# Two-layer hybrid decoder trunk: the first layer's x in buffers of its own, loaded by ScalarE's and GpSimd's queues

## The chip, the core and the metric

The kernel runs on one core of one Trainium2 chip. The metric is the device time of one execution in microseconds (us). Before the change three runs gave 2683.25 us as their median (2682.66 to 2684.56).

The core's engines are TensorE (PE; its weight loads are shown as PEld), VectorE (DVE), ScalarE (ACT), GpSimd (POOL) and SyncE (SP). Each executes its own instructions in the order that the program fixed, and they wait for each other by semaphores. A transfer (DMA) is issued by an engine's queue and moved by 16 DMA engines that all queues share.

## What is computed

Two decoder layers on a residual stream x of 256 tokens by 2048 features, float32:

```
for l in range(DEPTH):
    mix = hybrid_mixer(x, ...)                      # w_in projections: u, q, k, v, two gates
    x = layer_norm(DEEPNORM_ALPHA * x + mix, ...)   #   branch A: differential attention, 8 heads, causal
    h = square(relu(x @ w_mlp_up[l])) @ w_mlp_down[l]   # branch B: diagonal complex SSM, then GLU
    x = layer_norm(DEEPNORM_ALPHA * x + h, ...)     #   merged = gate_a * (attn @ w_attn_up) + gate_s * (ssm @ w_ssm_up)
```

Products are made in a split form. Each float32 operand becomes a high part, rounded to the matmul's type, and a low part, the remainder; a product is the sum of high x high, high x low and low x high.

## The kernel before

**Weights.** A weight chunk is 256 rows by 512 columns (512 KB). `load` (L331) takes a raw buffer from a ring of 4 (`RAW_BUFS`), issues the transfer on SyncE's queue (L337), and lets `split` (L141) make two tiles of it: `whi` on ScalarE (L142) and `wlo`, which needs `whi`, on VectorE (L144). `whi` and `wlo` come from rings of 3 (`HL_BUFS`), so the split of chunk n waits until TensorE has finished chunk n-3. `load_next` does this for the next chunk of a fixed plan.

**The first x.** The transposed x arrives as four pieces `c` of 512 features (512 KB each); piece 0 is cut into three transfers. Before the change, each piece took a buffer of the same ring of 4 raw buffers and the transfers stood on SyncE's queue, alternating with the first weight chunks (L422 to L431). `split` turns a piece into a tile `xT`, high on ScalarE, low on VectorE. The first projection (`gemm_feat`, L533, matmuls in L544 to L546) works through 8 weight chunks; chunks 2c and 2c+1 need piece c. A chunk is 24 matmuls.

**Background work.** Generators (`bg`) are pumped between chunks: tables for rotary embedding and SSM parameters (`rope_gen`, `ssm_param_gen`), the SSM scan (`ssm_gen`) and attention (`attn_gen`, L772). Small inputs are loaded by a list `drip` (L436), one transfer on GpSimd's queue for each finished chunk (L459).

**Attention's end.** `attn_gen` works on four pairs of heads. For each pair TensorE transposes the probabilities (L811), ScalarE copies them (`wT`, L812), TensorE multiplies with v (L817 to L819), ScalarE squares and sums (L823), VectorE makes an inverse root in some ten small operations (L825 and `rsqrt`, L319 to L327), ScalarE scales (L830), TensorE transposes back (L835), and the result is split into `ahl`: high on ScalarE (L838), low on VectorE (L839). Two pairs share an `ahl` tile. Behind the gates' projection, `w_attn_up` (`gemm_tok`, matmuls in L469, L470, L473) reads `ahl`: of the 4 chunks of each 512 output columns, the last needs the fourth pair. A chunk is 12 matmuls here.

**What sets the order.** The code above emits instructions; the order of each engine's list is then fixed by a list scheduler in the build, which works with its own model of the engines and can put an instruction ahead of ones that were emitted earlier. What is emitted early in the program can so move what stands much later.

Of the kernel before, what the change touches and what calls it, by code (L numbers as in the profile page):

```python
# [11 lines left out]
F32 = mybir.dt.float32  # L12
F32R = mybir.dt.float32r
BF16 = mybir.dt.bfloat16
I32 = mybir.dt.int32
AF = mybir.ActivationFunctionType
ALU = mybir.AluOpType
# [3 lines left out]
P = 128  # L21
# [9 lines left out]
L = 64  # L31
# [6 lines left out]
RAW_BUFS = 4  # L38
# [22 lines left out]
TURN = 6.283184  # L61
# [43 lines left out]
def trunk(ctx: ExitStack, tc: tile.TileContext, A, out):  # L105
    nc = tc.nc
    V, SC, GP, PE = nc.vector, nc.scalar, nc.gpsimd, nc.tensor
# [4 lines left out]
    wpool = ctx.enter_context(tc.tile_pool(name="wpool", bufs=3))  # L112
# [6 lines left out]
    def nm(s):  # L119
        uid[0] += 1  # L120
        return f"{s}_{uid[0]}"

    def slot(shape, dt=F32, name="slot"):
        return slots.tile(shape, dt, tag="slot", name=nm(name))
# [13 lines left out]
    def const(shape, name, dt=F32):  # L138
        return keep.tile(shape, dt, tag=name, name=name)

    def split(hi, lo, src, scale=1.0):  # L141
        SC.activation(hi, src, AF.Copy, scale=scale)  # L142
        if scale == 1.0:
            V.tensor_tensor(lo, src, hi.bitcast(F32), op=ALU.subtract)  # L144
        else:
            V.scalar_tensor_tensor(lo, src, scale, hi.bitcast(F32), op0=ALU.mult, op1=ALU.subtract)
# [13 lines left out]
            self.last = i  # L160

    bg = Background()

    ident = const([P, P], "ident")
    make_identity(nc, ident)
    ident16 = const([P, P], "ident16", BF16)
    GP.tensor_copy(ident16, ident)
    mask = const([P, 2, P], "mask", BF16)
    GP.memset(mask, 0.0)
    GP.affine_select(mask, mask, pattern=[[0, 2], [-1, P]], compare_op=ALU.is_ge, fill=-1e30, base=0, channel_multiplier=1)  # L170
    quarter = const([P, 1], "quarter")
    GP.memset(quarter, TURN / 4)
    steps = const([P, L], "steps")
    GP.iota(steps, pattern=[[1, L]], base=1, channel_multiplier=0, allow_small_or_imprecise_dtypes=True)

    dram = ctx.enter_context(tc.tile_pool(name="dram", bufs=1, space=bass.MemoryType.DRAM))
    xkeep = A["x"].rearrange("(t p) d -> t p d", p=P)
# [154 lines left out]
    def load(w, c, halves=False):  # L332
        kn, wn = w.shape[-2:]
        raw = wpool.tile([P, kn, wn], F32, tag="w", name=nm("w"), bufs=RAW_BUFS)
        parts = [slice(0, 1), slice(1, 2)] if halves else [slice(0, kn)]
        for k in parts:
            nc.sync.dma_start(raw[:, k], w[c][:, k])  # L337
        hi = wpool.tile([P, kn, wn], F32R, tag="whi", name=nm("whi"), bufs=HL_BUFS)
        lo = wpool.tile([P, kn, wn], F32R, tag="wlo", name=nm("wlo"), bufs=HL_BUFS)
        for k in parts:  # L340
            split(hi[:, k], lo[:, k], raw[:, k])
        return hi, lo

    def load_next(halves=False):
        w, c = plan.pop(0)
        ready.append((w, c, *load(w, c, halves=halves)))
# [52 lines left out]
    def weights(key, l, *idx):  # L399
        k = (key, l) + idx  # L400
        if k not in wts:
            wts[k] = A[key][(l,) + idx]
        return wts[k]

    for l in range(DEPTH):
# [11 lines left out]
        for key, *idx in order:  # L417
            w = weights(key, l, *idx)
            plan += [(w, c) for c in range(w.shape[0])]

    xT = []
    for c in range(4):  # L422
        raw = wpool.tile([P, 4, 256], F32, tag="w", name=nm("xraw"), bufs=RAW_BUFS)
        t = slot([P, 4, 2, 256], F32R, "xT")
        xT.append(t)
        parts = [slice(0, 1), slice(1, 2), slice(2, 4)] if c == 0 else [slice(0, 4)]
        for i, k in enumerate(parts):
            nc.sync.dma_start(raw[:, k], A["xT"][c][:, k])
            split(t[:, k, 0, :], t[:, k, 1, :], raw[:, k])
            if (c, i) in ((0, 0), (0, 2), (1, 0), (2, 0)):  # L430
                load_next(c == i == 0)  # L431

    def banks(shape):
        return [psg.tile(shape, F32, tag="g", name=nm("g")) for _ in range(2)]
# [66 lines left out]
    def boundary(ps, w, act, evac, stat, w2, normalizer, evac2):  # L501
        got = [take(w, c) for c in range(8 - TAIL, 8)]
        held = [take(w2, c) for c in range(HEAD)]
        mm, vd, va = Chain(), Chain(), Chain()
        tiles = [slot([P, 4, 2, 256], F32R, "xT") for _ in range(4)]
        act2 = from_tiles(tiles)
        ps2 = None
        for step in ORDER:
            what, tt, c = step[:-2], int(step[-2]), int(step[-1])
            if what == "tail":  # L510
                tok_mul(mm, ps, act, NKT, got[c], 8 - TAIL + c, tt)
            elif what == "evac":
                evac(tt, ps[tt], vd)
            elif what == "stat":
                stat(tt, vd)
            elif what == "head":
                if ps2 is None:
                    ps2 = banks([P, W])
                tok_mul(mm, ps2, act2, NKT, held[c], c, tt)
            else:  # L520
                normalizer(what, mm, vd, va, tt, c, tiles[c])
        for c in range(HEAD, NKT // 2):
            hl = fetch(w2, c)
            for tt in range(2):
                tok_mul(free, ps2, act2, NKT, hl, c, tt)
            bg.pump(rate[0])
        for tt in range(2):
            evac2(tt, ps2[tt])
        return tiles
# [406 lines left out]
    for l in range(DEPTH):  # L936
# [28 lines left out]
        def v_evac(n):  # L965
            return lambda tt, ps: SC.activation(v[:, tt, n * W:n * W + W], ps, AF.Copy)

        if l > 0:
            xT = boundary(*prev, weights("w_in", l, G_V), ln, v_evac(0))
# [235 lines left out]
```

## Time and profile before

| what | value |
|---|---|
| median of three runs | 2683.25 us |
| the profiled execution, own time | 2682.85 us |
| its span in the profile | 2681.1 us |
| TensorE busy | 2642.8 us (99%) |
| VectorE busy | 1909.8 us (71%) |
| ScalarE busy | 1308.3 us (49%) |
| GpSimd busy | 139.4 us (5%) |
| mean granted TensorE clock | 0.996 of full speed |

The span runs from the first to the last instruction; the execution's own time has some 1.8 us more around it. "Granted clock" is the share of TensorE's full 2.4 GHz that it was allowed; 0.5 is its lower level, 1.2 GHz. In the timeline's rows stand the start, the duration, engine, line, operation, output<-inputs and the shapes; in brackets the engine's idle time just before and what ended it.

### The profile page before, as it was taken

The numbers are of one execution on the slowest core, as the hardware profiler recorded it, in microseconds if no ns is written. First come the engines' busy times: TensorE is split into PE (matmuls) and PEld (weight loads), VectorE is DVE, ScalarE is ACT, GpSimd is POOL, SyncE is SP. The second block draws the span as 40 slices with busy tenths as digits, with TensorE's granted clock in tenths as the row PEclk, the third lists the DMA queues.
The fourth block names the chain that finished last, engine by engine and source line by source line (L and its number), as shares of the span: only waits on it lengthen the run. The fifth ranks groups of instructions, "written<-read, shape, count | busy, mean of one in ns | idle before, by whom it ended". The sixth has DMA issues, their size and how long they took to land. (4 is left out here: it accounts for less than half of the span.)

```text
span 2681.1 us, 37176 instructions
## 1 busy us (share of the span) xinstructions
PE 2642.8 (99%) x14144; PEld 2250.5 (84%) x14144; DVE 1909.8 (71%) x2685; ACT 1308.3 (49%) x1756; POOL 139.4 (5%) x289
## 2 busy tenths in 40 slices
PE   8999999999999999999999999999999999999998
PEld 8988878888888888888899878778888888888886
DVE  7899899666765576655659899878676655556556
ACT  5565554444554454543445555544445534435442
POOL 1101100000000000000011100001010000000000
PEclk9999999999999999999999999999999999999999
DMA  8756655674655676666577556557746665555673
GB/s 300 221 169 195 200 181 181 208 247 130 209 189 189 221 229 208 213 200 200 204 232 227 190 177 195 178 161 239 247 143 196 189 196 189 189 196 188 190 245 130
DMA packets 148947, 535.69 MB, mean 200 GB/s; under 512 B 18688, under 2 KB 18976, under 8 KB 147744
## 3 DMA queue, kind: packets, MB, share of 16 engines
q1 hardware_dynamic: 133488, 482.40, 55.7%
q0 software_dynamic: 15280, 50.91, 6.2%
q8 instruction: 111, 1.82, 0.3%
q14 instruction: 68, 0.56, 0.1%
HBM read 517.52 MB, written 15.73 MB: 199 GB/s over the span
## 5 line engine op out<-in xcount | busy, mean ns | idle before, releaser
L144 DVE TENSOR_TENSOR wlo<-w,whi 128x1024 fp32r<-128x1024 f32 (+1 forms) x884 | 1077.2, 1220 | 610.7 <-ACT whi L142 610.2
L142 ACT ACTIVATE whi<-w 128x1024 fp32r<-128x1024 f32 (+1 forms) x884 | 934.6, 1058 | 1035.6 <-PE g L473 649.0
L567 PE MATMUL g<-xT,whi 128*128 128x512 f32 x1920 | 654.4, 395 | 0.0
L567 PE MATMUL g<-xT,wlo 128*128 128x256 f32 x1920 | 496.9, 279 | 0.0
L567 PEld LDWEIGHTS g<-xT,whi 128*128 128x128 f32 x1920 | 344.4, 188 | 64.1
L567 PEld LDWEIGHTS g<-xT,wlo 128*128 128x128 f32 x1920 | 361.5, 188 | 20.8 <-DVE wlo L144 0.3
L470 PE MATMUL g<-wlo,hT 128*128 128x512 f32 x972 | 378.2, 389 | 0.0
L469 PE MATMUL g<-whi,hT 128*128 128x512 f32 x972 | 378.2, 389 | 0.0
L473 PE MATMUL g<-whi,hT 128*128 128x512 f32 x972 | 299.1, 389 | 0.0
L470 PE MATMUL g<-wlo,xT 128*128 128x512 f32 x680 | 268.3, 395 | 1.5 <-DVE wlo L144 1.5
L469 PE MATMUL g<-whi,xT 128*128 128x512 f32 x680 | 267.0, 395 | 1.3 <-ACT whi L142 1.3
L544 PE MATMUL g<-xT,whi 128*128 128x256 f32 x768 | 216.7, 286 | 5.8 <-ACT whi L142 5.8
L545 PE MATMUL g<-xT,whi 128*128 128x256 f32 x768 | 216.7, 285 | 0.0
L469 PEld LDWEIGHTS g<-whi,hT 128*128 128x128 f32 x972 | 182.5, 188 | 38.0
L470 PEld LDWEIGHTS g<-wlo,hT 128*128 128x128 f32 x972 | 182.4, 188 | 37.9
L473 PEld LDWEIGHTS g<-whi,hT 128*128 128x128 f32 x972 | 182.4, 188 | 37.8
L546 PE MATMUL g<-xT,wlo 128*128 128x256 f32 x768 | 211.2, 286 | 2.3 <-DVE wlo L144 2.3
L473 PE MATMUL g<-whi,xT 128*128 128x512 f32 x680 | 212.3, 392 | 0.0
L544 PEld LDWEIGHTS g<-xT,whi 128*128 128x128 f32 x768 | 149.0, 194 | 6.1 <-ACT whi L142 6.0
L470 PEld LDWEIGHTS g<-wlo,xT 128*128 128x128 f32 x680 | 128.2, 189 | 28.2 <-DVE wlo L144 2.6
L469 PEld LDWEIGHTS g<-whi,xT 128*128 128x128 f32 x680 | 128.4, 189 | 27.0 <-ACT whi L142 2.1
L473 PEld LDWEIGHTS g<-whi,xT 128*128 128x128 f32 x680 | 127.4, 188 | 27.1 <-issue 0.4
(292 smaller groups left out, 3196.6 us busy)
## 6 DMA issues: line engine op xcount, KB each, us to landing
w<-in_w_in_dram SPq DMA_DIRECT2D x253, 512.0 KB, 3.8
w<-in_w_mlp_down_dram SPq DMA_DIRECT2D x243, 512.0 KB, 3.5
w<-in_w_mlp_up_dram SPq DMA_DIRECT2D x240, 512.0 KB, 3.6
w<-in_w_out_dram SPq DMA_DIRECT2D x54, 512.0 KB, 4.2
w<-in_w_attn_up_dram SPq DMA_DIRECT2D x32, 512.0 KB, 3.6
w<-in_w_ssm_up_dram SPq DMA_DIRECT2D x32, 512.0 KB, 3.7
us<-usplit POOLq DMA_DIRECT2D x64, 128.0 KB, 4.9
bs<-bsplit POOLq DMA_DIRECT2D x64, 128.0 KB, 4.7
```

What stands on the lines that cost most here:

```text
L142: SC.activation(hi, src, AF.Copy, scale=scale)
L144: V.tensor_tensor(lo, src, hi.bitcast(F32), op=ALU.subtract)
L469: mm(PE.matmul(ps[tt], act(kt)[:, 0, ts], hi[:, k, :], start=kt == 0, stop=False))
L470: mm(PE.matmul(ps[tt], act(kt)[:, 0, ts], lo[:, k, :], start=False, stop=False))
L473: mm(PE.matmul(ps[tt], act(kt)[:, 1, ts], hi[:, k, :], start=False, stop=kt == nkt - 1))
L544: m(PE.matmul(o, wh, ah, start=first and b % 2 == 0, stop=False))
L545: m(PE.matmul(o, wh, al, start=False, stop=False))
L546: m(PE.matmul(o, wl, ah, start=False, stop=last and b % 2 == 1))
L567: mm[j](PE.matmul(o, wt, mv, start=kt == 0 and i == 0, stop=last and i == 1))
```

## The change

The first x no longer uses the weights' raw ring. It gets two raw buffers of its own from the pool of 17 large slots, two pieces in each. Its transfers leave SyncE's queue: the first quarter of piece 0 is issued by ScalarE, everything else by GpSimd. The constants that GpSimd makes (identity matrices, causal mask, a quarter turn, step numbers) stood at the program's start and are now emitted behind this loop.

```diff
 bg = Background()
-
-    ident = const([P, P], "ident")
-    make_identity(nc, ident)
-    ident16 = const([P, P], "ident16", BF16)
-    GP.tensor_copy(ident16, ident)
-    mask = const([P, 2, P], "mask", BF16)
...
-    steps = const([P, L], "steps")
-    GP.iota(steps, pattern=[[1, L]], base=1, channel_multiplier=0, allow_small_or_imprecise_dtypes=True)
...
     xT = []
+    xraw = [slot([P, 2, 4, 256], name="xraw") for _ in range(2)]
     for c in range(4):
-        raw = wpool.tile([P, 4, 256], F32, tag="w", name=nm("xraw"), bufs=RAW_BUFS)
+        raw = xraw[c // 2][:, c % 2]
         t = slot([P, 4, 2, 256], F32R, "xT")
         xT.append(t)
         parts = [slice(0, 1), slice(1, 2), slice(2, 4)] if c == 0 else [slice(0, 4)]
         for i, k in enumerate(parts):
-            nc.sync.dma_start(raw[:, k], A["xT"][c][:, k])
+            (nc.scalar if c == i == 0 else GP).dma_start(raw[:, k], A["xT"][c][:, k])
             split(t[:, k, 0, :], t[:, k, 1, :], raw[:, k])
             if (c, i) in ((0, 0), (0, 2), (1, 0), (2, 0)):
                 load_next(c == i == 0)
+
+    ident = const([P, P], "ident")
...
+    GP.iota(steps, pattern=[[1, L]], base=1, channel_multiplier=0, allow_small_or_imprecise_dtypes=True)
```

The scheduler's order differs from the one before on every engine up to the first layer's GLU, and is the same after it. Lines behind the removed block have other numbers in the changed file: the split stays L142 and L144, a weight's transfer is L325 instead of L337, the x transfers are L417 instead of L428, and from L433 on a line is one higher (L811 becomes L812, L835 becomes L836). Numbers at the end of names count buffers.

**Place 1: GpSimd, the transfers of the first 30 us.** `ss<-in_pos` is a small input of the drip list and waits for TensorE to finish weight chunk 1; it is so before and after. Before:

```order
masks.py:199 AFFINE_SELECT ident<-ident 128x128
L174 IOTA steps 128x64
L170 AFFINE_SELECT mask<-mask 128x256
L167 CAST ident_81<-ident 128x128
L459 DMA ss_95<-in_pos_dram 128x256
L459 DMA inv<-in_inv_dram 128x2
L459 DMA prm_94<-in_ssm_p_dram 128x192
L459 DMA lqk_100<-in_lqk_dram 128x512
```

and now, the two last transfers of piece 0 standing right ahead of these rows:

```order
L417 DMA xraw_94<-in_xT_dram 128x1024
masks.py:197 MEMSET ident 128x128
L427 MEMSET mask 128x256
L430 MEMSET quarter 128x1
L432 ISA
L432 IOTA steps 128x64
masks.py:199 AFFINE_SELECT ident<-ident 128x128
L428 AFFINE_SELECT mask<-mask 128x256
L425 CAST ident_150<-ident 128x128
L460 DMA ss_79<-in_pos_dram 128x256
L417 DMA xraw_95<-in_xT_dram 128x1024 x2
L460 DMA inv<-in_inv_dram 128x2
```

The transfers of pieces 2 and 3 (`xraw_95`) stand behind `ss<-in_pos` and so behind its wait.

**Place 2: ScalarE, the splits that the first projection needs.** Before, `xT_111`, `xT_137`, `xT_148` and `xT_159` are the pieces 0 to 3, and `whi_154`, `whi_249`, `whi_283`, `whi_330` the chunks 3 to 6:

```order
L142 ACTIVATE xT_137<-xraw_136 128x4x256
L142 ACTIVATE whi_143<-w_141 128x1024
L142 ACTIVATE xT_148<-xraw_147 128x4x256
L142 ACTIVATE whi_154<-w_152 128x1024
L142 ACTIVATE xT_159<-xraw_158 128x4x256
L142 ACTIVATE whi_249<-w_247 128x1024
L142 ACTIVATE whi_283<-w_281 128x1024
L142 ACTIVATE whi_330<-w_328 128x1024
```

Now, with `xT_121`, `xT_131`, `xT_141` the pieces 1 to 3 and `whi_137`, `whi_247`, `whi_281`, `whi_328` the chunks 3 to 6:

```order
L142 ACTIVATE whi_137<-w_135 128x1024
L142 ACTIVATE xT_121<-xraw_94 128x4x256
L142 ACTIVATE whi_247<-w_245 128x1024
L142 ACTIVATE whi_281<-w_279 128x1024
L142 ACTIVATE whi_328<-w_326 128x1024
L142 ACTIVATE xT_131<-xraw_95 128x4x256
L142 ACTIVATE xT_141<-xraw_95 128x4x256
L142 ACTIVATE whi_374<-w_372 128x1024
```

Piece 2, which chunk 4 needs, was split ahead of the weights of chunk 3; it now stands behind those of chunk 6. VectorE's list has the same new sequence for the low parts.

**Place 3: TensorE, the last pair of heads in the first layer.** `aux_3379` before and `aux_3377` now are the transposes of that pair's second head, whose copy is the start of the pair's last chain. Before, they stand among the gates' matmuls, which read `xT`:

```order
L473 MATMUL g_4304<-whi_4395,xT_148 128x512 x2
L469 MATMUL g_4303<-whi_4414,xT_148 128x512
L811 MATMUL aux_3379<-ident,at_3316 128x128
L817 MATMUL aux_3384<-v_168,wT_3241 128x128
L818 MATMUL aux_3384<-v_168,wT_3241 128x128
L811 MATMUL aux_3379<-ident,at_3316 128x128 x2
L819 MATMUL aux_3384<-v_168,wT_3241 128x128
L470 MATMUL g_4303<-wlo_4415,xT_148 128x512
```

and now:

```order
L474 MATMUL g_4302<-whi_4448,xT_141 128x512 x2
L470 MATMUL g_4484<-whi_4466,ahl_2540 128x512
L812 MATMUL aux_3377<-ident,at_3314 128x128
L818 MATMUL aux_3382<-v_166,wT_3239 128x128
L819 MATMUL aux_3382<-v_166,wT_3239 128x128
L812 MATMUL aux_3377<-ident,at_3314 128x128 x2
L820 MATMUL aux_3382<-v_166,wT_3239 128x128
L471 MATMUL g_4484<-wlo_4467,ahl_2540 128x512
```

Before, 35 matmuls of the gates and then 72 of `w_attn_up` that do without the fourth pair follow these transposes; now the gates are finished, and 71 of `w_attn_up` follow. In the second layer, whose order is the same before and after, 11 of the gates and 72 of `w_attn_up` follow them.

## Rows read from the trace of the kernel before

**Rows 1.** The page: the span, and TensorE's part 1.

```profile
span 2681.1 us, 37176 instructions
...
PE 2642.8 (99%) x14144; PEld 2250.5 (84%) x14144; DVE 1909.8 (71%) x2685; ACT 1308.3 (49%) x1756; POOL 139.4 (5%) x289
```

**Rows 2.** Waits of TensorE, 0 to 31 us: total us, times, longest.

```profile
PE g L544 <- ACT whi L142: 5.8, 2, 4.8
PE g L546 <- DVE wlo L144: 1.2, 3, 0.5
```

**Rows 3.** Waits of TensorE, 1738 to 1772 us (second layer's attention end).

```profile
PE g L470 <- DVE wlo L144: 1.8, 3, 0.9
PE g L469 <- ACT ahl L838: 1.7, 1, 1.7
PE aux L835 <- ACT at L830: 1.4, 1, 1.4
```

**Rows 4.** Waits of TensorE, 403 to 434 us (first layer's attention end).

```profile
PE g L470 <- DVE wlo L144: 1.7, 1, 1.7
```

**Rows 5.** Timeline, one wait of TensorE in the SSM at 110 us.

```profile
112.71 1.04 PE L710 MATMUL bu<-us,bs 128*128 128x256 f32 x4 [2.59 <-DMA us<-usplit]
```

**Rows 6.** Stretches: length; PE, PEld, DVE, ACT, POOL busy (instructions); PEclk; DMA share; GB/s.

```profile
112.90:116.30 3.40, 3.40 (x17) 3.40 (x17) 2.98 (x5) 0.00 (x0) 2.09 (x4) 0.50 0.65 186
116.30:119.70 3.40, 3.40 (x31) 3.40 (x30) 3.08 (x5) 1.06 (x1) 0.00 (x0) 1.00 0.91 222
1753.00:1764.90 11.90, 8.72 (x35) 5.85 (x34) 11.90 (x27) 4.35 (x8) 0.00 (x0) 1.00 0.58 186
1764.90:1771.70 6.80, 5.42 (x13) 4.26 (x14) 5.83 (x9) 1.33 (x3) 0.00 (x0) 0.50 0.23 77
```

**Rows 7.** Timeline, the head, 0 to 31 us.

```profile
0.74 0.39 SPq L428 DMA_DIRECT2D xraw<-in_xT_dram  x1
...
4.82 0.58 PE L544 MATMUL g<-xT,whi 128*128 128x256 f32 x1 [4.82 <-ACT whi L142]
...
13.43 0.69 POOL L459 DMA_DIRECT2D ss<-in_pos_dram  x1 [11.13 <-PE g L546]
...
16.76 1.06 ACT L142 ACTIVATE xT<-xraw 128x1024 fp32r<-128x1024 f32 x1 [0.47 <-DMA xraw<-in_xT_dram]
...
19.84 1.22 DVE L144 TENSOR_TENSOR xT<-xraw,xT 128x1024 fp32r<-128x1024 f32 x1
...
21.25 0.38 PE L544 MATMUL g<-xT,whi 128*128 128x256 f32 x1 [1.00 <-ACT whi L142]
```

**Rows 8.** DMA issues: KB each, median us from issue to landing; `braw` with its range.

```profile
ss<-in_pos_dram POOLq DMA_DIRECT2D x1, 128.0 KB, 6.2
braw<-in_bT_dram POOLq DMA_DIRECT2D x8, 256.0 KB, 5.4
DMA to landing us min/median/max: 4.2/5.4/8.3
```

**Rows 9.** Timeline, the last pair's chain in the first layer.

```profile
404.19 0.27 PE L811 MATMUL aux<-ident,at 128*128 128x128 f32 x1
...
414.38 0.39 PE L469 MATMUL g<-whi,ahl 128*128 128x512 f32 x1
...
426.13 0.40 PE L470 MATMUL g<-wlo,ahl 128*128 128x512 f32 x1
426.36 0.39 PE L469 MATMUL g<-whi,ahl 128*128 128x512 f32 x1
...
428.49 0.67 ACT L838 ACTIVATE ahl<-aux,gsub 128x512 fp32r<-128x512 f32 x1
```

**Rows 10.** Timeline, the last pair's chain in the second layer.

```profile
1738.66 0.27 PE L811 MATMUL aux<-ident,at 128*128 128x128 f32 x1
...
1765.56 0.67 ACT L838 ACTIVATE ahl<-aux,gsub 128x512 fp32r<-128x512 f32 x1
...
1767.50 0.74 DVE L839 SCALAR_TENSOR_TENSOR ahl<-aux,gsub,ahl 128x512 fp32r<-128x512 f32 x1
```

More of the change, by code (lines that the diff above doesn't have):

```diff
@@ L162, in trunk @@
     bg = Background()
-    ident = const([P, P], "ident")
-    make_identity(nc, ident)
-    ident16 = const([P, P], "ident16", BF16)
-    GP.tensor_copy(ident16, ident)
-    mask = const([P, 2, P], "mask", BF16)
[L169 to L172, printed above, removed]
-    steps = const([P, L], "steps")
-    GP.iota(steps, pattern=[[1, L]], base=1, channel_multiplier=0, allow_small_or_imprecise_dtypes=True)
     dram = ctx.enter_context(tc.tile_pool(name="dram", bufs=1, space=bass.MemoryType.DRAM))
@@ L431, in trunk @@
                 load_next(c == i == 0)
+    ident = const([P, P], "ident")
+    make_identity(nc, ident)
+    ident16 = const([P, P], "ident16", BF16)
+    GP.tensor_copy(ident16, ident)
+    mask = const([P, 2, P], "mask", BF16)
+    GP.memset(mask, 0.0)
+    GP.affine_select(mask, mask, pattern=[[0, 2], [-1, P]], compare_op=ALU.is_ge, fill=-1e30, base=0, channel_multiplier=1)
+    quarter = const([P, 1], "quarter")
+    GP.memset(quarter, TURN / 4)
+    steps = const([P, L], "steps")
+    GP.iota(steps, pattern=[[1, L]], base=1, channel_multiplier=0, allow_small_or_imprecise_dtypes=True)
     def banks(shape):
```

## The prediction

> **What bounds the kernel.** I read the page first. TensorE is busy 2642.8 of 2681.1 us [rows 1], so some 38 us of the span are not its own, and the change can only cost or give what it alters in TensorE's waiting and clock. Then the waits of TensorE, stretch by stretch. In the head it waits 4.8 us for the first weights and, once started, 1.0 us more for ScalarE (5.8 less 4.8) and 1.2 us for VectorE: 2.2 us in all [rows 2]. At the end of attention it waits 1.8 + 1.7 + 1.4 = 4.9 us in the second layer [rows 3], but only 1.7 us in the first [rows 4]. In the SSM there is one wait of 2.59 us for a transfer [rows 5]. The table of stretches shows what such waits cost on top: behind the 2.59 us the granted clock is 0.50, the 1.2 GHz level, for 3.4 us, in which 17 matmuls start where the next 3.4 us hold 31; that gives away half of 3.4, 1.7 us. Behind the waits of the second layer's attention it is 0.50 for 6.8 us, of which TensorE works 5.42: 2.7 us given away. In the 11.9 us ahead of that, VectorE is busy without a gap: the end of attention is a race between VectorE's list and the matmuls that can go ahead without the last pair of heads [rows 6].
>
> So the question is not how fast x arrives, but whether the new order makes TensorE wait more in the head, and which of the two shapes the end of the first layer's attention takes.
>
> **Edits that cost nothing.** GpSimd's constants now follow three transfers; their readers, attention's transposes and the SSM's tables, come long after the first projection's first chunks, which hide the shift. The two slots for raw x are free again once piece 3 is split. ScalarE issues one transfer ahead of its table load; SyncE's queue needed 0.39 us for the same issue [rows 7], and ScalarE stands idle there until data has landed. The first matmul starts at 4.82 us behind the first half chunk's split. Its transfer moves up by that one issue, but the first x piece must now be split behind it on ScalarE, a quarter of a piece where a whole one takes 1.06, so I leave 4.8 us as it is. Without the cover the price would be some 0.4 us.
>
> **The head.** Before, ScalarE splits piece 2 ahead of chunk 3's weights, and TensorE enters chunk 4 at 21.25 us, after 1.00 us of waiting [rows 7]. Now the list puts the split of piece 2 behind `whi` of chunk 6. The ring of `whi` holds three, so that split waits until TensorE has finished chunk 3. Only then come `whi` (1.06 us, the same size as the split in the row at 16.76), piece 2's high part (1.06 us) and, on VectorE, its low part, whose 1.22 us begin behind a `wlo` of the same length. TensorE meanwhile has nothing but two matmuls of chunk 4. Chunk 3 ends at about 20 us (before: 20.25, waits included). The high part is there 1.06 + 1.06 = 2.1 us later and the low part some 1.2 us after that: 3.2 us of waiting with the two matmuls taken off. The same sequence in small at chunk 2 (piece 1 behind chunk 3's weights) costs some 0.4 us. Against this stand the 2.2 us of waits that the old order had. Head: 3.6 - 2.2 = **+1.4 us**.
>
> This holds if piece 2 has landed by 21 us. It is issued behind `ss<-in_pos`, which left GpSimd at 13.43 us when chunk 1 ended [rows 7], so at about 14. That small transfer took 6.2 us to land and a 256 KB `braw` on the same queue 4.2 to 8.3 us [rows 8], which puts piece 2, twice as long, anywhere between 18.2 us and 14 + 8.3 = 22.3, and with a `braw`'s further step for the second half about 23.2. So the head's upper end is 2.2 us higher. I take 21 or earlier, nearer to the middle of the rows, so that ScalarE's list decides. The Trainium skill ("DMA: Bandwidth & Descriptors", "Anatomy of one DMA - SWDGE (gpsimd) path") gives a fixed 2.0 us plus bytes over 436 GB/s, by which 512 KB would take an estimated 3.2 us. The trace does not agree: 128 KB took 6.2 us here; by the page the head would keep its lower value for certain, by the rows it may rise by 2.2 us.
>
> The new wait is as long as the 2.59 us after which the clock fell for 3.4 us, so I add that row's 1.7 us. Head with clock: **+3.1 us**, between +1.4 and +5.3.
>
> **The end of the first layer's attention.** From the last pair's transposes to the end of its high part takes 429.16 - 404.19 = 25.0 us [rows 9] in the first layer and 1766.23 - 1738.66 = 27.6 us in the second [rows 10]. Behind the transposes the first layer's order has 107 matmuls that need nothing of this pair (35 of the gates, 72 of `w_attn_up`); at 0.23 us each (from 426.13 to 426.36, [rows 9]) they last 24.6 us, and TensorE waited only the 1.7 us for another reason. The second layer has 83, or 19.1 us, and waited 4.9. After the change the first layer has 71, or 16.3 us: 12 fewer than the second, 2.8 us less cover. The work on VectorE's list between those points is the same. By the second layer's rows TensorE then waits 4.9 + 2.8 = 7.7 us; with the first layer's shorter chain, 2.6 us less, 5.1. I take 7.7, because the new order of TensorE has the second layer's shape (gates finished when the chain begins). Less the 1.7 us of before, that is **+6.0 us**; the low end is +3.4, and the high end +8.4, if the chain's first VectorE step comes another 2.4 us later (a `wlo` and two of the SSM's operations ahead of it). The second layer's clock row adds 2.7 us: **+8.7 us**.
>
> **Between them.** The 2.59 us wait in the SSM sits between two groups of its matmuls with 54 projection matmuls in the middle; in the new order there are 48, at 3.4 us for 31 [rows 6] 0.7 us less cover. So I expect it again, 0.7 us longer: **+0.7 us**. Other waits of a few tenths in the first layer will come and go with the new order. Their bounds are the loss of this wait with its clock, -4.3, and as much as the head's small waits again, +2.2.
>
> **The sum** against the profiled execution's 2682.85 us: 3.1 + 8.7 + 0.7 = 12.5, so **2695 us**. That execution lies 0.4 us below the median of 2683.25, which changes nothing. A measurement of this kernel can tell about 0.2% from no change, 5.4 us, so "slower" begins at 2688.6.
>
> **Rivals.**
>
> *The cover holds.* The chain on VectorE may run earlier against the matmuls than the counts say, since the whole of the first layer is shuffled and the SSM's share of VectorE can have moved away from it. Then only the head is left: 2682.85 + 3.1 = 2686, no change that can be told. For it: in the first layer before, 25.0 us met 24.6 us of cover. Against it: the chain would have to shrink from 25.0 us to 16.3, and VectorE has no idle time there to shrink into. The same time results if the move of the queues does only what the Trainium skill says of it ("DMA: Bandwidth & Descriptors", "Issuing engines are not separate DMA queues": all queues share the same 16 DMA engines, only issue time is saved). The trace agrees in so far as that issue time was 0.39 us a transfer. Chance 0.12.
>
> *The SSM's transfer comes in time.* If x away from SyncE and the new places of GpSimd's transfers let the `us` data land ahead of its matmuls, the 2.59 us and the clock's 1.7 us are saved, and with the old head's 2.2 us of waits gone the kernel gains 6.5 us: 2676. It decides where the landing takes under 5.3 us from the buffer's release (48 x 3.4 / 31). Against it: the cover between the groups shrinks, and the head's splits stand in the wrong order. Chance 0.04.
>
> *All upper ends together:* head +5.3, attention 8.4 + 2.7, between +2.9: 19.3, so 2702. Chance 0.12.
>
> **How the numbers follow.** My forecast has the remaining 0.72. The case in which only the head is left ends under 2688.6 and is the whole of "no change", with a tail of the forecast's low end (head +1.4, attention +3.4, no fall of the clock: 2688) of 0.02. So faster 0.04, same 0.14, slower 0.82. The range goes from 2686, which takes in the first rival, to 2703, above the upper case; outside are the fast rival and the tails.
>
> **What would show it.** Right: a wait of TensorE of 2 us or more for ScalarE's split of x at chunk 4, near 20 us, then one of about 1 us for its low part; `xraw` on GpSimd behind `ss<-in_pos`; waits of 6 to 9 us in sum around 415 to 440 us, the longest at the transposes in L836 or at `ahl`, with the clock at 0.50 behind them; from the first layer's GLU on the same waits as before. Wrong: no wait at L836 in the first layer (the cover held), or the SSM's wait at 110 us gone, or the two pieces of x landing later than 23 us, which would push the head beyond +5.

## The result and the profile after

| | before | the change |
|---|---|---|
| median | 2682.66 us (5 runs, 2680.30 to 2684.56) | 2698.68 us (5 runs, 2694.53 to 2699.68) |
| ratio | | 1.0058, 95% interval 1.0047 to 1.0069 |
| profiled execution, own time | 2682.85 us | 2695.32 us |
| its span | 2681.1 us | 2693.5 us |

The change makes the kernel slower by 16.0 us in the medians and by 12.5 us between the profiled executions. The forecast was 2695, between 2686 and 2703. The page of the kernel after:

```profile
span 2693.5 us, 37165 instructions
...
PE 2645.0 (98%) x14144; PEld 2250.7 (84%) x14144; DVE 1908.2 (71%) x2685; ACT 1307.4 (49%) x1756; POOL 142.0 (5%) x294
```

Against [rows 1], TensorE's share of the span that is not its own grew from 2681.1 - 2642.8 = 38.3 to 2693.5 - 2645.0 = 48.5 us: 10.2 of the 12.4 us are waiting. The other 2.2 us are the same 14144 matmuls taking longer. The work itself did not change, so the question is where TensorE waits.

**The head.** TensorE's waits from 0 to 31 us (total us, times, longest):

```profile
PE g L545 <- ACT xT L142: 8.3, 3, 4.9
PE g L546 <- DVE xT L144: 1.7, 2, 0.9
```

Without the first 4.9 us, which the kernel before has too (4.8), that is 5.1 us; before it was 2.2 [rows 2]. The timeline of the same stretch (start, duration, engine, line, operation; in brackets the idle time before and what ended it):

```profile
10.68 0.51 PE L545 MATMUL g<-xT,whi 128*128 128x256 f32 x2 [0.67 <-ACT xT L142]
12.02 0.39 PE L546 MATMUL g<-xT,whi 128*128 128x256 f32 x1 [0.84 <-DVE xT L144]
...
15.82 0.57 POOL L460 DMA_DIRECT2D ss<-in_pos_dram  x1 [11.27 <-PE g L547]
16.40 1.06 POOL L417 DMA_DIRECT2D xraw<-in_xT_dram  x2
...
22.08 1.06 ACT L142 ACTIVATE whi<-w 128x1024 fp32r<-128x1024 f32 x1 [1.82 <-PE g L546]
23.78 1.06 ACT L142 ACTIVATE xT<-xraw 128x1024 fp32r<-128x1024 f32 x1 [0.64 <-DMA xraw<-in_xT_dram]
...
24.89 0.51 PE L545 MATMUL g<-xT,whi 128*128 128x256 f32 x2 [2.73 <-ACT xT L142]
26.24 0.58 PE L546 MATMUL g<-xT,whi 128*128 128x256 f32 x1 [0.85 <-DVE xT L144]
```

Read from the bottom: TensorE waits 2.73 us at chunk 4 for piece 2's high part. ScalarE could not split it earlier, because ahead of it in its list stands `whi` of chunk 6, and that one waits until TensorE has left chunk 3 (22.08). When ScalarE is free again, at 23.14, the piece is still 0.64 us away. It was issued behind `ss` and its wait, at 16.40. So the list holds the piece back first, and the transfer a little longer still.

**The end of the first layer's attention.** TensorE's waits from 419 to 455 us:

```profile
PE aux L836 <- ACT at L831: 4.2, 1, 4.2
PE g L470 <- ACT ahl L839: 2.5, 1, 2.5
PE g L471 <- DVE wlo L144: 2.0, 2, 1.2
```

8.7 us, where [rows 4] has 1.7. The second layer's three waits are the same as in [rows 3]. The timeline shows the last pair's chain, with some of VectorE's rows between the steps:

```profile
420.02 0.27 PE L812 MATMUL aux<-ident,at 128*128 128x128 f32 x1
...
431.12 0.16 DVE L826 TENSOR_SCALAR ss<-ss 128x4 f32<-128x4 f32 x1
...
432.47 1.22 DVE L144 TENSOR_TENSOR wlo<-w,whi 128x1024 fp32r<-128x1024 f32 x1
...
434.21 0.15 DVE L315 SCALAR_TENSOR_TENSOR rs<-rsa,rs 128x4 f32<-128x4 f32 x1
434.28 2.33 DVE L736 TENSOR_TENSOR_SCAN sw<-ss,sw 128x512 f32<-128x512 f32 x2
436.53 0.14 DVE L313 TENSOR_TENSOR rsa<-rs 128x4 f32<-128x4 f32 x1
...
444.20 0.15 DVE L315 SCALAR_TENSOR_TENSOR rs<-rsa,rs 128x4 f32<-128x4 f32 x1
...
444.81 1.10 PE L836 MATMUL aux<-ident,at 128*128 128x128 f32 x4 [4.16 <-ACT at L831]
...
447.72 0.67 ACT L839 ACTIVATE ahl<-aux,gsub 128x512 fp32r<-128x512 f32 x1
448.44 0.80 PE L470 MATMUL g<-whi,ahl 128*128 128x512 f32 x1 [2.53 <-ACT ahl L839]
```

From the transposes to the end of the high part pass 448.39 - 420.02 = 28.4 us. The inverse root is eleven operations of some 0.15 us each, 1.7 us of work, but they lie between 431.12 and 444.35, among the SSM's scans and the weights' splits. TensorE meanwhile runs out of matmuls that do without this pair.

**The clock** behind these waits (length; PE, PEld, DVE, ACT, POOL busy; PEclk; DMA share; GB/s):

```profile
12.40:15.80 3.40, 3.40 (x19) 3.40 (x18) 3.27 (x3) 2.01 (x2) 0.00 (x0) 0.50 0.80 214
26.05:29.45 3.40, 3.21 (x15) 3.21 (x16) 3.40 (x14) 0.07 (x1) 0.00 (x0) 0.50 0.88 301
445.90:452.70 6.80, 4.27 (x11) 3.39 (x11) 5.27 (x8) 1.48 (x3) 0.00 (x0) 0.50 0.12 49
1780.50:1783.90 3.40, 3.40 (x9) 2.67 (x9) 3.29 (x6) 0.00 (x0) 0.00 (x0) 0.50 0.34 140
```

Not all of this is extra. Before, there were such stretches at 112.9 and, for 6.8 us, in the second layer [rows 6], and one from 1519.2 to 1522.6 us. Now those at 112.9 and 1519.2 are gone and the second layer's is the last row above, half as long. On balance TensorE's busy time grew by 2.2 us.

**Between them.** TensorE's waits from 85 to 130 us:

```profile
PE g L547 <- DVE wlo L144: 2.2, 3, 1.0
PE bu L711 <- DMA us<-usplit: 0.9, 1, 0.9
PE bu L711 <- issue: 0.7, 1, 0.7
PE bu L711 <- DVE wlo L144: 0.5, 1, 0.5
```

The one wait of 2.59 us [rows 5] fell apart into several of under 1.1 us.

### The profile page after: what moved, and what is told of

It reads as the page before. It is cut to its first block, busy times and chain, and to the rows that moved or that the text cites. A ratio compares the mean times of both kernels' runs of the same rounds, so it can differ in the third digit from the quotient of the medians.

```text
span 2693.5 us, 37165 instructions
## 1 busy us (share of the span) xinstructions
PE 2645.0 (98%) x14144; PEld 2250.7 (84%) x14144; DVE 1908.2 (71%) x2685; ACT 1307.4 (49%) x1756; POOL 142.0 (5%) x294
## 5 line engine op out<-in xcount | busy, mean ns | idle before, releaser
L144 DVE TENSOR_TENSOR wlo<-w,whi 128x1024 fp32r<-128x1024 f32 (+1 forms) x884 | 1076.8, 1220 | 618.2 <-ACT whi L142 617.2
L142 ACT ACTIVATE whi<-w 128x1024 fp32r<-128x1024 f32 (+1 forms) x884 | 934.5, 1058 | 1047.9 <-PE g L474 653.8
L568 PEld LDWEIGHTS g<-xT,whi 128*128 128x128 f32 x1920 | 344.4, 188 | 64.1
L568 PEld LDWEIGHTS g<-xT,wlo 128*128 128x128 f32 x1920 | 361.5, 188 | 20.7 <-DVE wlo L144 0.2
L545 PEld LDWEIGHTS g<-xT,whi 128*128 128x128 f32 x768 | 149.0, 194 | 8.8 <-ACT xT L142 8.7
L546 PEld LDWEIGHTS g<-xT,whi 128*128 128x128 f32 x768 | 149.7, 195 | 2.8 <-DVE xT L144 2.4
L547 PEld LDWEIGHTS g<-xT,wlo 128*128 128x128 f32 x768 | 146.1, 195 | 4.6 <-DVE wlo L144 4.0
```

The costliest lines, as they stand in the source:

```text
L545: m(PE.matmul(o, wh, ah, start=first and b % 2 == 0, stop=False))
L546: m(PE.matmul(o, wh, al, start=False, stop=False))
L547: m(PE.matmul(o, wl, ah, start=False, stop=last and b % 2 == 1))
L568: mm[j](PE.matmul(o, wt, mv, start=kt == 0 and i == 0, stop=last and i == 1))
```

## The experiments

The theory: the lists' new order costs the time, at two places. In the head the pieces of x are split too late; at the end of attention the last pair's chain has fewer matmuls to hide it. Rivals: the transfers themselves (another queue, a later landing), the move of the constants, the buffers. Ratios are to the kernel before on the same chip, with 95% intervals.

| kernel | median us | ratio | interval |
|---|---|---|---|
| x_scalar_queue | 2677.34 | 0.9980 | 0.9970 to 0.9989 |
| constants_late | 2684.22 | 1.0001 | 0.9992 to 1.0009 |
| own_buffers | 2680.48 | 0.9992 | 0.9984 to 1.0001 |
| x_moved_constants_early | 2689.57 | 1.0024 | 1.0015 to 1.0033 |
| x_before_ss | 2682.94 | 1.0003 | 0.9994 to 1.0012 |
| attention_end_first | 2686.91 | 1.0018 | 1.0009 to 1.0027 |
| scalar_head_in_order | 2687.16 | 1.0024 | 1.0015 to 1.0033 |
| queues_only | 2688.03 | 1.0023 | 1.0014 to 1.0032 |
| root_on_gpsimd | 2699.16 | 1.0067 | 1.0054 to 1.0081 |
| scalar_queue_root_on_gpsimd | 2686.32 | 1.0013 | 1.0005 to 1.0022 |
| last_root_on_gpsimd | 2693.89 | 1.0051 | 1.0038 to 1.0063 |
| scalar_queue_last_root_on_gpsimd | 2679.03 | 0.9986 | 0.9977 to 0.9995 |

### One part of the change alone

**constants_late** has the constants behind the loop and x as before:

```diff
-        raw = xraw[c // 2][:, c % 2]
+        raw = wpool.tile([P, 4, 256], F32, tag="w", name=nm("xraw"), bufs=RAW_BUFS)
...
-            (nc.scalar if c == i == 0 else GP).dma_start(raw[:, k], A["xT"][c][:, k])
+            nc.sync.dma_start(raw[:, k], A["xT"][c][:, k])
```

> The constants are made behind the loop as in the change; x keeps the weights' ring and SyncE's queue. Theory (order): TensorE's, ScalarE's and VectorE's lists are those of before, so 2680 to 2686 us and the waits of before. Rival (the constants' move starts a delay of GpSimd's work that reaches attention): 2688 us or more.

The ratio is 1.0001. But this run tests less than it seems: the scheduler puts the constants back to where they were, and GpSimd makes them from 0.73 to 2.30 us, as before the change. All engines' lists are those of before, so the run is a second measurement of one and the same order. That is useful too. Its head waits 7.7 + 0.5 - 4.5 = 3.7 us, 1.5 more than before: at chunk 4 TensorE waits 2.37 us instead of 1.00, because ScalarE waits for that chunk's transfer. So much can two profiles of one order differ in the head. Constants that are really made later, behind three transfers of x (from 2.97 us on), stand in the change and in x_before_ss below.

**own_buffers** has the two slots for raw x and the constants at the start; of the transfers it takes back the queues:

```diff
-            (nc.scalar if c == i == 0 else GP).dma_start(raw[:, k], A["xT"][c][:, k])
+            nc.sync.dma_start(raw[:, k], A["xT"][c][:, k])
...
```

> Own buffers alone: two large slots for raw x, transfers on SyncE's queue, constants at the start. Theory (order): behind the last pair's transposes stand 25 of the gates' matmuls and 61 of w_attn_up's ahead of the first wait for the pair, 97 in all against 94 before, so about 2 us of waiting there, and up to 2 us more in the head: 2681 to 2688 us. Rival (two of the 17 slots missing, or a weights' ring freed of x that lets the weights run ahead, delay the first layer): 2692 us or more.

0.9992, with the median just under the expected range, and 1.4 us of waiting from 400 to 450 us, none of it for the pair. The buffers cost nothing.

**queues_only** has the new queues, with the constants at the start and the weights' ring:

```diff
-        raw = xraw[c // 2][:, c % 2]
+        raw = wpool.tile([P, 4, 256], F32, tag="w", name=nm("xraw"), bufs=RAW_BUFS)
...
```

> Queues alone: x on ScalarE's and GpSimd's queues, but in the weights' ring of raw buffers and with the constants at the start. Theory (order): at the attention end the second layer's shape again, 11 and 72 matmuls, so 4 to 6 us of waits there; in the head 2 to 5 us, as the pieces are split late; 2686 to 2695 us. Rival (own buffers or late constants are needed for the loss): 2680 to 2685 us.

**x_moved_constants_early** is the change with the constants left at the start:

```diff
     bg = Background()
...
+    ident = const([P, P], "ident")
...
-    ident = const([P, P], "ident")
...
```

> x as in the change (own buffers, ScalarE's and GpSimd's queues), constants at the start. Theory (order): behind the last pair's transposes stand 11 of the gates' and 72 of w_attn_up's matmuls, the second layer's shape, so 4 to 6 us of waiting there with the clock low behind it; in the head the second half of piece 0 is split behind chunk 3's weights, some 2 us of waiting at about 10 us, and none over 1.5 us at 20 us. 2687 to 2696 us. Rival (the transfers themselves, x arriving late on GpSimd's queue, make the loss): the same as the change within 3 us, 2696 to 2702 us, with waits for x ended by transfers.

Both times came out in the theory's range, at 1.0023 and 1.0024. The waits at the end of attention are 3.9 and 3.8 us, just under the expected 4, and the low clock behind them did not come. So moving x to ScalarE's and GpSimd's queues is the part that costs, and it costs only some 6 us by itself. The full 16 need the constants emitted late as well, which alone change no list. Costs that belong to the parts would add up; these don't. What the parts set together is the order.

### Undo the order, keep the change

**x_scalar_queue** leaves SyncE's queue too, but for ScalarE's alone:

```diff
-            (nc.scalar if c == i == 0 else GP).dma_start(raw[:, k], A["xT"][c][:, k])
+            nc.scalar.dma_start(raw[:, k], A["xT"][c][:, k])
```

> The change, but all six transfers of x stand on ScalarE's queue and none on GpSimd's; own buffers and the late constants stay. Theory (the order of the lists): here piece 2 is split ahead of chunk 6's weights and 35 of the gates' matmuls stand behind the last pair's transposes again, as before the change. So no wait over 1 us for piece 2 near 20 us, about 1.7 us of waiting at the first layer's attention end, and 2680 to 2687 us. Rival (taking x off SyncE's queue, or its own buffers and late constants, cost by themselves): 2692 us or more, most of the 16 us stay.

Its page:

```profile
span 2674.5 us, 37172 instructions
...
PE 2638.7 (99%) x14144; PEld 2246.9 (84%) x14144; DVE 1909.4 (71%) x2685; ACT 1307.5 (49%) x1756; POOL 139.2 (5%) x289
```

and the waits of its head, 0 to 31 us:

```profile
PE g L545 <- ACT whi L142: 4.9, 1, 4.9
PE g L546 <- DVE xT L144: 0.5, 1, 0.5
```

Nothing is left in the head but 0.5 us, and between 400 and 450 us there is the one wait of 1.7 us as before. This kernel is faster than before, by 5.9 us in the medians (2683.24 before on that chip), and so below the range that the theory had expected. Idle time of TensorE is 35.8 us against 38.3 before; the other part is TensorE's busy time, 2638.7 against 2642.8, with fewer stretches of low clock (mean 0.998 against 0.996).

**x_before_ss** pins one thing: GpSimd issues pieces 2 and 3 ahead of the first two small inputs.

```diff
-            (nc.scalar if c == i == 0 else GP).dma_start(raw[:, k], A["xT"][c][:, k])
+            last_x = (nc.scalar if c == i == 0 else GP).dma_start(raw[:, k], A["xT"][c][:, k])
...
-            tc.add_manual_dep(GP.dma_start(dst, src).ins, i.name, behind, reason="spread transfers")
+            d = GP.dma_start(dst, src).ins
+            tc.add_manual_dep(d, i.name, behind, reason="spread transfers")
+            if len(drip) in (5, 6):
+                tc.add_manual_dep(d, last_x.ins.name, after, reason="order")
```

> The change with one thing pinned: GpSimd issues pieces 2 and 3 of x ahead of the first two small inputs and their waits. The lists then have piece 1 split behind chunk 3's weights, piece 2 behind chunk 5's instead of chunk 6's, and behind the last pair's transposes 35 of the gates' matmuls stand again, as before the change. Theory (the order of the lists, at both places): no wait over 1 us for piece 2 near 22 us but 2 to 4 us for piece 1 near 15 us; at the first layer's attention end about 1.7 us and none at L836; 2683 to 2691 us. Rival 1 (x on GpSimd's queue lands late by itself): waits for x ended by its transfers, 2692 us or more. Rival 2 (the head alone makes the loss): with 4 us or more of waits left in the head, 2695 us or more.

GpSimd's transfers in its timeline:

```profile
1.24 1.75 POOL L417 DMA_DIRECT2D xraw<-in_xT_dram  x3 [0.80 <-POOLq L1200]
...
4.49 1.10 POOL L417 DMA_DIRECT2D xraw<-in_xT_dram  x2
...
14.92 0.54 POOL L460 DMA_DIRECT2D ss<-in_pos_dram  x1 [9.33 <-PE g L550]
```

and TensorE's waits from 400 to 450 us:

```profile
PE g L474 <- DVE wlo L144: 1.7, 1, 1.7
```

With everything of the change kept, and two transfers issued 12 us earlier, a stall 400 us further on is gone and the time is that of before. That is the clearest of the runs for the theory: the queue is GpSimd's all the same, and the constants are as late. Its head still waits as long as the change's, 7.8 + 2.1 - 4.9 = 5.0 us, only at other chunks. So rival 2, the head alone, falls as well. The head's waits are not free for that: in its profile TensorE idles 2681.6 - 2639.7 = 41.9 us, 3.6 more than before, and is busy 3.1 us less, as fewer stretches had the low clock.

### The two places apart

**attention_end_first** marks two parts of the chain for the list as of high priority, from VectorE's root to the scaling and from the transposes back to the split:

```diff
+            with tc.high_priority():
...
```

> The change with the end of each pair's chain (VectorE's root, scaling, transposes back, split) marked as of high priority for the list. The head's lists are the change's; behind the last pair's transposes now stand 47 of the gates' matmuls and 48 of w_attn_up's ahead of its first reader, 101 in all against 78. Theory (cover): the head waits as in the change, about 5 us with 2.7 at chunk 4; the attention end 2 to 4 us instead of 8.7, no 4 us wait at the transposes, no low clock of 6.8 us behind it; 2686 to 2693 us. Rival (the loss is in the head and the SSM, the attention end follows whatever its cover): 2695 us or more.

1.0018, inside the expected range. Waits from 400 to 450 us:

```profile
PE g L471 <- DVE wlo L144: 1.1, 2, 0.8
PE g L470 <- ACT ahl L841: 1.1, 1, 1.1
```

The head is the change's (7.6 + 1.9 - 4.8 = 4.7 us) and its list too. There piece 2 had landed when ScalarE came to it, and TensorE still waited 1.98 + 0.94 us at chunk 4: the list alone is enough for that wait.

**scalar_head_in_order** binds ScalarE's first splits to the order of the code:

```diff
-        SC.activation(hi, src, AF.Copy, scale=scale)
+        a = SC.activation(hi, src, AF.Copy, scale=scale)
+        if hseq[0]:
+            hseq[0](a)
...
+    hseq[0] = Chain()
...
+    hseq[0] = None
```

> The change with ScalarE's first splits bound to the order of the code: every piece of x ahead of the weights that are loaded behind it. The list then also issues pieces 2 and 3 ahead of the small inputs, and at the attention end it has the second layer's shape, 11 of the gates' matmuls and 72 of w_attn_up's. Theory (order, two separate places): the head 2 to 4 us of waits, most of it for low parts near 17 us; the attention end 4 to 6 us of waits with the clock low behind it; 2686 to 2694 us. Rival (the head alone makes the loss): 2680 to 2685 us.

1.0024. The head waits 5.0 + 2.5 - 4.8 = 2.7 us. From 400 to 450 us:

```profile
PE g L480 <- DVE ahl L846: 1.5, 1, 1.5
PE g L476 <- ACT ahl L845: 1.3, 1, 1.3
PE g L477 <- DVE wlo L148: 1.0, 1, 1.0
```

Queues_only and x_moved_constants_early show the same three waits, to 0.1 us. Set side by side, with the matmuls of the gates and of `w_attn_up` that stand in TensorE's list between the last pair's transposes and the first one that reads the pair's `ahl`:

| matmuls as cover | kernel | waits for the pair | ratio |
|---|---|---|---|
| 97 | own_buffers | 0 | 0.9992 |
| 96 | before; x_before_ss | 0 | 1; 1.0003 |
| 96 | attention_end_first | 1.1 us | 1.0018 |
| 83 | the three of this shape | 2.8 to 2.9 us | 1.0023 to 1.0024 |
| 71 | the change | 4.2 + 2.5 = 6.7 us | 1.0058 |

The 96 of before are 35 of the gates and 61 of `w_attn_up`. The other 11 of the 72 that do without the fourth pair stand behind its first reader and cover nothing, so the 107 counted ahead of the result was too high. From 96 to 83 the cover loses 13 matmuls of 0.23 us, 3.0 us, and the waits are 2.8 to 2.9. From 83 to 71 it loses 2.8 us more, and the waits grow by 3.8 to 3.9. The count alone does not settle it: before and attention_end_first have the same 96, but before has its 1.7 us wait for `wlo` inside that stretch, which gives the chain that much more time. Nor is the ratio the cover's alone, for the heads differ: they wait 1.4 us in own_buffers, 2.7 to 5.5 in the three, about 5 in attention_end_first and the change.

### Can the chain be shortened?

**root_on_gpsimd** moves the root's three rounds to GpSimd:

```diff
+            (E or V).tensor_tensor(a, o, o, op=ALU.mult)
+            if E:
+                E.tensor_tensor(a, a, v, op=ALU.mult)
+                E.tensor_scalar(a, a, -0.5, 1.5, op0=ALU.mult, op1=ALU.add)
+                E.tensor_tensor(o, o, a, op=ALU.mult)
...
-            rsqrt(rs, ss, 4)
+            rsqrt(rs, ss, 4, GP)
```

> The change with attention's inverse root off VectorE: behind its first two steps the three rounds are made by GpSimd, 12 operations in place of VectorE's 9. The head's lists are the change's. Theory (the last pair's chain is long because its ten root operations of 0.15 us each stand between VectorE's splits and scans, 13 to 14 us from the first to the last in both layers): the root takes 4 to 7 us, the chain some 8 us less, and the waits for the last pair go in both layers: 8.7 to under 3 us in the first, 4.9 to under 2 in the second, with the low clock behind them; 10 to 18 us less than the change, 2681 to 2689 us, the head's 5 us stay. Rival (only the cover counts, or GpSimd's small operations queue behind its transfers and are as late): within 4 us of the change, 2694 us or more.

**scalar_queue_root_on_gpsimd** has the same edit in x_scalar_queue.

> All x transfers on ScalarE's queue, and attention's root on GpSimd: the two edits that should take away the head's waits and those of both attention ends. Theory: 5 to 9 us less than with the queue alone (4.9 us of the second layer's waits and the low clock behind them, 1.7 to 2.7), 2668 to 2674 us. Rival (as for the root alone, GpSimd as late as VectorE): 2675 to 2680 us.

Both missed: 1.0067 and 1.0013. The waits for the last pair are gone in both layers, as expected, but now the earlier pairs are waited for. In root_on_gpsimd, 200 to 390 us:

```profile
PE aux L841 <- ACT at L836: 6.0, 2, 3.4
```

and behind those two waits (columns as above):

```profile
237.20:240.60 3.40, 3.40 (x10) 2.25 (x8) 2.60 (x4) 1.71 (x2) 0.00 (x0) 0.50 0.23 19
360.10:366.90 6.80, 6.80 (x19) 4.88 (x19) 5.67 (x9) 3.42 (x6) 0.00 (x0) 0.50 0.26 81
```

The second layer has 3.4 us of the same waits. TensorE's idle time is 2.8 us less than in the change (2696.9 - 2651.2 = 45.7 against 48.5), its busy time 6.2 us more (2651.2 against 2645.0), with the mean clock at 0.993 against 0.995. The mistake was to think of the last pair alone. The new list puts earlier pairs' transposes back closer behind their root: the first pair's start 11.4 us behind the root's start, a wait of 3.4 us included (224.91 to 236.30), against 21.5 without a wait in the change (225.95 to 247.42). GpSimd's operations take longer than that leaves room for. Part of its root for that pair:

```profile
227.03 4.05 POOL L313 TENSOR_TENSOR rsa<-rs 128x4 f32<-128x4 f32 x1 [9.03 <-DVE rs L307]
...
232.85 1.03 POOL L313 TENSOR_TENSOR rsa<-rs 128x4 f32<-128x4 f32 x1
...
234.81 0.20 POOL L313 TENSOR_TENSOR rsa<-rs 128x4 f32<-128x4 f32 x1
```

**last_root_on_gpsimd** keeps the earlier pairs on VectorE, and **scalar_queue_last_root_on_gpsimd** does so in x_scalar_queue:

```diff
-            rsqrt(rs, ss, 4, GP)
+            rsqrt(rs, ss, 4, GP if hp == 3 else None)
```

> The change with the inverse root on GpSimd for the last pair of heads alone; the first three pairs keep theirs on VectorE, so their waits (6.0 us in the first layer, 3.4 in the second with all roots on GpSimd) should not be there. The head is the change's. With all on GpSimd its operations took 0.20 us alone and up to 4.05 beside VectorE's, in the mean about 0.5, so twelve of them 6 us against 13 to 14 on VectorE. Theory (chain against cover): the last pair's chain is some 7 us shorter, but the first layer's list puts its transposes back earlier, behind 60 instead of 71 matmuls; waits there 8.7 to 3 to 6 us, in the second layer 4.9 to 2 to 4; 2686 to 2695 us. Rival (the waits of the earlier pairs or GpSimd's lock eat it all again): 2697 us or more.

> All x transfers on ScalarE's queue, and the last pair's root alone on GpSimd. Theory: against the queue alone (2677) the second layer's 4.9 us of waits shrink to 2 to 4 and the low clock behind them by half or all of its 1.7 us; the first layer stays within 1 us: 2673 to 2677 us. Rival (GpSimd beside VectorE is as slow as VectorE's own list): 2678 to 2682 us.

The earlier pairs' waits are gone, and still nothing is gained that these runs can tell. The first comes to 1.0051, an interval that overlaps the change's; its time is in the expected range, but its waits are not: 4.1 + 1.6 + 2.5 = 8.2 us in the first layer and 5.5 in the second. The second comes to 2679.03, the rival's range, with this in the second layer (1738 to 1772 us):

```profile
PE aux L841 <- ACT at L836: 4.5, 1, 4.5
PE g L476 <- DVE wlo L144: 1.0, 2, 0.7
```

In the change with this edit the root goes from 435.46 to 443.53 on GpSimd, after two steps on VectorE from 433.94: 9.6 us instead of 13.2, and the first layer's list lets the transposes follow 11 matmuls earlier. The wait stays; why 3.6 us less of root gain nothing beyond these 11 matmuls (some 2.5 us) is not shown. The lowest ratio of the study is x_scalar_queue's, which the runs cannot tell from scalar_queue_last_root_on_gpsimd's.

## Why the prediction was right

The likeliest case came true: slower, 2695.32 us in the profiled execution against a forecast of 2695, and 2698.68 in the median. Both places and the mechanism, the order of the lists, were right. That the profiled execution hits the sum to the microsecond is luck. Of the forecast's 12.5 us, 1.4 + 6.0 + 0.7 = 8.1 are waits and 1.7 + 2.7 = 4.4 the clock; measured are 10.2 us of idle time and 2.2 of longer matmuls, two misses of about 2 us that cancel. Against the median's 16.0 us the sum is 3.5 short. The steps:

- **The head, waits +1.4.** Measured 5.1 - 2.2 = +2.9. The wait at chunk 4 was right in place and size: 2.73 + 0.85 = 3.6 us for 3.2 forecast. The small one of 0.4 us at chunk 2 did not come. Instead there are 0.67 + 0.84 = 1.5 us at 10 to 12 us, where the second half of piece 0 is split behind chunk 1's weights; the prediction has no term for that.
- **Piece 2 landed by 21 us.** This assumption failed. TensorE left chunk 1 at 15.8 us and not at about 14, so `ss` and the pieces behind it were issued 2 us later, and piece 2 landed at 23.78, some 7.4 us after its issue and past the forecast's upper bound of 23.2. This is one of the prediction's own signs of being wrong, and the head with its clock did come out beyond +5. But the landing has only a small part in it, 0.64 us, because chunk 3 ended late too; the rest is the wait at 10 to 12 us and a second stretch of low clock.
- **The head's clock, +1.7.** There were two stretches at 0.50 and not one, which give away half of 3.40 + 3.21, 3.3 us; the head with its clock is +6.2. With the very same lists such stretches come and go: constants_late has one from 22.6 to 26.0 us where before has none, and none at 1519.2 where before has one. So the term is good to a stretch or two.
- **The end of attention, waits +6.0.** Measured 8.7 - 1.7 = +7.0. The race of cover against chain was right, and the kernels with 71 to 97 matmuls of cover bear it out. The 107 matmuls, 24.6 us, that the prediction gives the first layer before the change were 96, some 22 us; the sum does not hang on them, as it starts from the second layer's 83, which is the right count. The chain was taken as the second layer's 27.6 us and measured 28.4; that is most of the missing 1.0.
- **Its clock, +2.7.** 6.8 us at 0.50, of which TensorE worked 4.27: 2.1 us given away. What the forecast left out is that stretches elsewhere went, at 1519.2 us and half of the second layer's.
- **The SSM, +0.7.** Wrong in form, and near 0 in sum: between 85 and 130 us the waits are 4.3 us, in pieces, 1.7 more than the 2.6 of before, but the low clock at 112.9 us, which gave away 1.7 us, did not come.
- **The rivals.** "The cover holds" fell with the 4.2 us wait at L836, and "the SSM's transfer in time" with the sum. Of the first, the remark that queues save issue time only is borne out as far as the transfers go: x on GpSimd's queue costs nothing that the ratio of 1.0003 in x_before_ss shows. What costs is the order that is built around them.

The median lies 3.4 us above the profiled execution, which was the second shortest of five. From where in the kernel those 3.4 us come, no profile here shows.

## What to carry to other kernels

Where a scheduler builds the instruction lists, an edit to the first 20 us can put its cost 400 us away. Compare the lists and count what stands between a chain's start and its first reader, here 96 matmuls against 71, before asking whether a transfer lands in time. A transfer that is issued from a queue behind another instruction's wait inherits that wait, and so does all that the list then puts behind its data.

## What was not expected of the hardware

In root_on_gpsimd the same GpSimd operation on 128x4 values took 0.20 us at 234.81, where VectorE stood idle (from 233.90 to 238.00), and 4.05 us at 227.03, while VectorE executed two-input operations without a gap:

```profile
227.46 1.21 DVE L144 TENSOR_TENSOR wlo<-w,whi 128x1024 fp32r<-128x1024 f32 x1
228.59 0.68 DVE L750 TENSOR_TENSOR sw<-ss,ss 128x512 f32<-128x512 f32 x1
229.19 0.68 DVE L751 TENSOR_TENSOR sw<-sw,ss 128x512 f32<-128x512 f32 x1
229.80 1.21 DVE L144 TENSOR_TENSOR wlo<-w,whi 128x1024 fp32r<-128x1024 f32 x1
...
231.56 2.34 DVE L741 TENSOR_TENSOR_SCAN sw<-ss,sw 128x512 f32<-128x512 f32 x2
```

The long one ends at 231.08, where VectorE's splits and products end (231.01); the one of 1.03 us at 232.85 ends at 233.88, with the second of the two scans (231.56 + 2.34 = 233.90). The Trainium skill ("SBUF — State Buffer", "SBUF: two separate sides") says that these two engines lock a shared pair of ports for a whole instruction, VectorE's two-input operations included, and that the other one is then held entirely. The trace agrees in that both long operations end where VectorE's do. It shows more than that: the one of 4.05 us is held over several VectorE instructions in a row, the longest of which is 1.21 us. Why it does not get in between two of them, no run here shows. The profile's spans on GpSimd are rough, but the chain's next operation starts 4.13 us after this one (231.16).
